# A step of plain f's put ahead of the operand building, the building cut in two, and two weight sums given to POOL

## The chip, the cores and the metric

The kernel runs on one core of one Trainium2 chip. The metric is device time of one execution in microseconds (us), lower is better. The engines are called PE (matmuls, with PEld for its weight loads), DVE (vector), ACT (activations), POOL (GpSimd) and SP (which here only issues transfers).

## The reference

Two layers of a hybrid block on one sequence of 1024 tokens, 1024 features, in float32. A layer has a mixing part with four mixers side by side and a feed-forward part with a gate:

```python
def conv_ffn(h, w_up, conv_w, conv_b, w_down):
    a, b = jnp.split(h @ w_up, 2, axis=-1)
    a = causal_dwconv(a, conv_w) + conv_b.astype(a.dtype)
    return (jax.nn.gelu(a, approximate=True) * b) @ w_down

def hybrid_layer(x, ...):
    h = rms_norm(x, g_pre_mix)
    p = h @ w_in
    ...
    y = jnp.concatenate([y_a, y_b, y_c, y_d], axis=-1).astype(dt)
    x = x + rms_norm(y @ w_out, g_post_mix)
    h = rms_norm(x, g_pre_ffn)
    x = x + rms_norm(conv_ffn(h, w_up, conv_w, conv_b, w_down), g_post_ffn)
    return x
```

`D_FF` is 2816, which is 22 groups of 128 columns, called f's below (0 to 21).

## The kernel before, in words

**Precision.** A float32 operand x is kept as two reduced-precision tiles, hi = cast(x) (ACT) and lo = x - hi (DVE). A product is three matmuls: hi·hi, hi·lo and lo·hi.

**Tiles and halves.** The sequence is worked on in two halves of 512 tokens, each of 4 blocks of 128. Half 0 (the first) of a stage runs while half 1 is prepared, and so on. Instructions are written in a Python order, but a scheduler of the framework gives each engine its order at build time; each engine then works through its list strictly in that order and waits where a semaphore asks for it. Each DMA queue belongs to an engine and is in the engine's list: SP's holds weight loads and most stores, POOL's holds the loads `hn`, the stores to `hnD` and `gD`, and some norms' loads.

**The end of layer 1.** This is the place of the change. `out(l, 1, y, True)` is the second half's output projection (L235 to L237 are its matmuls), followed block by block by the norms (`norms`, L316 to L326). The tiles of the four blocks are called oqf, okt, org and osu. For each block: load of the residual `xb`, square and mean on ACT (`sumsq`, L309), a chain of nine small DVE operations for the inverse root (L280 to L288), L319 (scale), L320 (add to `xb`), a store of `xb` to `xs` by SP (L321), once more square and root, and L324, which gives the rows for the feed-forward part; POOL stores them to `hnD` (L326).

**The feed-forward part of the last layer** has two forms. Half 0 of f's 0 to 9 is done the plain way, by `plain_part`, a generator: each step does two f's (four weight units through `a_unit`, 24 matmuls each, L214 to L216, then gate and split), and the down products of the step before (`down`, 48 matmuls, L1054 to L1056, with the additions L1061); a sixth step does the last down products. One step is taken in the last mixing stage, `NMIX = 2` more before `out`, and the other three after the operands of half 1 are built.

The rest is done by products in Strassen's manner (Winograd's form, 7 products in place of 8): `build` makes the operands of one half from the stored rows. It works in two portions (`pairs` 0 and 1), each of two blocks: two loads `hn` (L1128), four sums on POOL (`sums`, L1103 to L1106, into `sa` and `sb`), 28 transposes on PE (L1112, four for each of the seven operands A11, S1, S2, A12, S3, Q4, A22), and for each operand a cast on ACT (L1118) and a subtraction on DVE (L1119). The tiles `hn`, `sa`, `sb` and the passes' `a` and `c` share one tag `c` with four buffers. `up_f(l, f, halves)` is a pass of one f over one half (84 matmuls, L1139, called a half-pass here) or over both (168, a full pass). It loads two weight tiles (`wraw`, three buffers), makes seven casts with their subtractions (L1154, L1155) and four sums of weights (L1159), all marked as urgent (`ahead=2000`), multiplies, gates (L1207 to L1212), and stores the gated row to `gD` by POOL (L1213). The f's 10 to 21 take full passes; f's 0 to 9 need half-passes for half 1 only. Before, f's 0 and 1 run, then both portions of half 0 are built, and the other eight half-passes stand between full ones.

Of the kernel before, what the change touches and what calls it, by code (L numbers as in the profile page):

```python
# [14 lines left out]
ALU = mybir.AluOpType  # L15
# [11 lines left out]
NF = 22  # L27
# [27 lines left out]
NA = 14  # L55
WS = 1056
FULL = (1,)
NPRE, NMIX = 10, 2

PM_DCW, PM_PSC, PM_SLG, PM_DNG, PM_ALOG, PM_DT, PM_PBD = 0, 24, 26, 28, 29, 33, 37  # L60
PM_N = 37 + 256
# [57 lines left out]
class Net:  # L119
# [1023 lines left out]
    def up_f(self, l, f, halves, ahead=2000):  # L1143
        nc, pf = self.nc, self.pf[l]
        V, cf = nc.vector, self.state[l]["cf"]
        n = len(halves)
        N = 256 * n
        rb, ra = (self.pu.tile([P, 2, 512], F32, tag="raw", name="wraw", bufs=3) for _ in range(2))
        for e, r in ((1, rb), (0, ra)):
            nc.sync.dma_start(r.rearrange("p q c -> p (q c)"), self.t["wU"][l, 2 * f + e])  # L1150

        def cast(x):
            w = self.pv.tile([P, 2, 512], F32R, tag="w", name="w", bufs=9)
            nc.scalar.copy(w[:, 0], x)  # L1154
            V.tensor_tensor(w[:, 1], x, w[:, 0].bitcast(F32), ALU.subtract)  # L1155
            return w

        def add(o, a):
            V.tensor_tensor(o, o, a, ALU.add)  # L1159

        with self.tc.high_priority(offset=ahead):
            b11, b21, b12, b22 = rb[:, 0], rb[:, 1], ra[:, 0], ra[:, 1]
            w11 = cast(b11)
            add(b11, b12)
            wt1 = cast(b11)
            w22 = cast(b22)
            add(b12, b22)
            add(b22, b11)
            wt2 = cast(b22)
            w21 = cast(b21)  # L1170
            wt3 = cast(b12)
            add(b21, b22)
            wt4 = cast(b21)
        X = self.ps()[:, :N]
        Z = self.pq()[:, :N]
        W = self.pq("h")[:, :N]
        p1, p5, u2 = (self.pbuf(x)[:, :N] for x in ("p1", "p5", "u2"))
        ab = self.cbuf("a")
        a = ab[:, 0:2 + 2 * N]
        c = self.cbuf("c")[:, :2 * N]  # L1180
        at = a[:, 2:].rearrange("p (b e t) -> p b e t", b=2 * n, e=2)
        ct = c.rearrange("p (b e t) -> p b e t", b=2 * n, e=2)
        v = lambda x: x.rearrange("p (b t) -> p b t", b=2 * n)
        w = lambda j: pf[:, PF_CW + 3 * f + j:PF_CW + 3 * f + j + 1]
        cb = pf[:, PF_CB + f:PF_CB + f + 1]
        if halves[0] == 0:
            nc.gpsimd.memset(a[:, 0:2], 0.0)
        else:
            nc.gpsimd.tensor_copy(a[:, 0:2], cf[:, f, :])
        self.product(X, "A11", w11, halves, True, False)  # L1190
        self.product(Z, "S1", wt1, halves, True, False)
        with self.tc.high_priority(offset=1500):
            nc.scalar.copy(p1, X)
            nc.scalar.copy(p5, Z)
        self.product(X, "S2", wt2, halves, False, False)
        self.product(W, "A12", w21, halves, True, True)
        with self.tc.high_priority(offset=1500):
            nc.scalar.copy(u2, X)
            V.tensor_tensor(p1, p1, W, ALU.add)
        self.product(X, "S3", wt3, halves, False, False)  # L1200
        self.product(Z, "Q4", w22, halves, False, True)
        with self.tc.high_priority(offset=1500):
            V.tensor_tensor(at[:, :, 1], v(p5), v(X), ALU.subtract)
            V.tensor_tensor(at[:, :, 0], v(Z), v(u2), ALU.subtract)
        self.product(X, "A22", wt4, halves, False, True)
        with self.tc.high_priority(offset=1500):
            nc.scalar.activation(c, a[:, 2:], AF.Identity, bias=cb, scale=w(2))  # L1207
            V.scalar_tensor_tensor(c, a[:, 1:1 + 2 * N], w(1), c, ALU.mult, ALU.add)
            V.scalar_tensor_tensor(c, a[:, 0:2 * N], w(0), c, ALU.mult, ALU.add)
            nc.scalar.activation(c, c, AF.Gelu_apprx_tanh)  # L1210
            V.tensor_tensor(ct[:, :, 0], ct[:, :, 0], v(p1), ALU.mult)
            V.tensor_tensor(ct[:, :, 1], ct[:, :, 1], v(X), ALU.mult)  # L1212
        nc.gpsimd.dma_start(self.gD[l][f, :, halves[0] * HALF:halves[0] * HALF + 2 * N], c)  # L1213

    def down_full(self, l):
        nc, t = self.nc, self.t
# [140 lines left out]
    def run(self):  # L1357
        hT = self.first_norm(0)
        y = self.win(0, 0, hT)
        hT = self.hT1  # L1360
        pre = self.early(0, 1, hT)
        acc = self.out(0, 0, y, halves=True)
        y = self.win(0, 1, hT, pre)
        for l in range(DEPTH - 1):
            acc = self.ffn_norm(l, 0, self.ffn(l, 0, self.to_hT(acc, True)))
            self.load_params(l + 1)
            hT = self.to_hT(acc)
            acc = self.out(l, 1, y)
            y = self.win(l + 1, 0, hT)
            acc = self.ffn_norm(l, 1, self.ffn(l, 1, self.to_hT(acc, True)))  # L1370
            hT = self.to_hT(acc)
            acc = self.out(l + 1, 0, y)
            keep = {}

            def fill(a=acc):
                keep["g"] = self.plain_part(l + 1, self.to_hT(a, True))
                next(keep["g"])

            y = self.win(l + 1, 1, hT, mid=fill)
        l = DEPTH - 1  # L1380
        part = keep["g"]
        for _ in range(NMIX):
            next(part)
        self.out(l, 1, y, True)
        self.A = {}
        self.layout("left", ("pu", 1), ("pA1", 1))
        self.rows(self.pA1, 1)
        self.build(l, 1)
        for _ in part:
            pass  # L1390
        self.layout("right", ("pA0", 1), ("pv", 9))
        self.rows(self.pA0, 0)
        for f in range(2):
            self.up_f(l, f, (1,))
        self.build(l, 0)
        half = list(range(2, NPRE))
        for f in range(NPRE, NF):
            if half:
                self.up_f(l, half.pop(0), (1,))
            self.up_f(l, f, (0, 1))  # L1400
        self.down_phase()
        self.down_full(l)
        for st in self.stacks.values():
            st.close()
# [77 lines left out]
```

## Time and profile before

| | us |
|---|---|
| median of 3 runs (lowest, highest) | 2557.81 (2556.66, 2564.56) |
| the profiled execution | 2557.59 |
| its span, first to last instruction | 2555.8 |
| PE busy | 2435.4 (95%) |
| DVE busy | 1809.1 (71%) |
| ACT busy | 983.0 (38%) |
| POOL busy | 272.0 (11%) |

The profile cuts the span in 40 slices of 63.9 us; each digit is the busy share of a slice in tenths. Mean granted TensorE clock over the span is 0.978. In the timeline a row has start, duration, engine, line, operation, output and input, shape, and in brackets how long the engine was idle before it and what ended that. A line number with L is a line of the kernel.

### The profile page before, as it was taken

What the parts mean: (1) busy time and instruction counts of PE and PEld (TensorE: products, weight loads), DVE (VectorE), ACT (ScalarE), POOL (GpSimd) and SP (SyncE); (2) the same over time, 40 slices, a digit from 0 to 9 for tenths busy, and PEclk for the clock granted to TensorE, in tenths of its full rate; (3) what the DMA queues carried; (4) which work ended last, traced back from release to release, by engine and by line L of the source; (5) the groups of instructions that cost most, each with busy time, mean ns of one, the idle gap of its engine ahead of it and who ended that gap; (6) DMA issues with size and microseconds to landing.
All of it is one profiled execution on the core that took longest, in us unless ns stands there. A gap on an engine that the chain in (4) does not pass through costs nothing.

```text
span 2555.8 us, 38925 instructions
## 1 busy us (share of the span) xinstructions
PE 2435.4 (95%) x15220; PEld 2093.1 (82%) x15220; DVE 1809.1 (71%) x3719; ACT 983.0 (38%) x1538; POOL 272.0 (11%) x389
## 2 busy tenths in 40 slices
PE   8989998999999999999999999999949799999998
PEld 7968987877788987787788898777838699999887
DVE  7895799765655898955665689976655777774747
ACT  5333452423332553332332355234432444443412
POOL 2321113000000013100000002211020200000000
PEclk9999998999999999999999999999969899999999
DMA  5233442322223552322222354222442332222723
GB/s 182 71 89 109 131 142 82 98 76 83 79 91 124 165 163 71 91 82 76 83 91 91 128 186 149 85 84 64 165 155 78 114 101 98 96 88 80 257 67 132
DMA packets 100221, 281.00 MB, mean 110 GB/s; under 512 B 30834, under 2 KB 31154, under 8 KB 99524
## 3 DMA queue, kind: packets, MB, share of 16 engines
q1 hardware_dynamic: 91428, 248.54, 30.7%
q0 software_dynamic: 8608, 29.96, 3.4%
q8 instruction: 120, 1.97, 0.3%
q14 instruction: 65, 0.53, 0.1%
HBM read 241.20 MB, written 37.26 MB: 109 GB/s over the span
## 4 chain that ended last, share of the span: by engine, by line
PE 75%; DVE 14%; DMA 4%; issue 4%; ACT 2%; POOL 1%; SPq 0%; DVEq 0%; ACTq 0%; POOLq 0%
PE psg L215 9%; PE psg L216 9%; PE psg L214 9%; PE psg L1139 7%; PE psm L1139 4%; PE psg L1297 3%; PE psg L1298 3%; PE psg L1299 3%; DVE pr L841 3%; PE psg L235 3%; PE psg L236 3%; PE psg L237 3%; DVE wlo L205 2%; PE psh L1139 2%; DVE A L843 1%
## 5 line engine op out<-in xcount | busy, mean ns | idle before, releaser
L216 PE MATMUL psg<-hT,wlo 128*128 128x512 f32 x1312 | 524.1, 401 | 0.0
L215 PE MATMUL psg<-hT,whi 128*128 128x512 f32 x1312 | 523.4, 399 | 0.2 <-DVE hT L373 0.2
L204 ACT CAST whi<-raw 128x1024 fp32r<-128x1024 f32 (+1 forms) x290 | 301.9, 1048 | 570.6 <-PE psg L215 229.0
L214 PE MATMUL psg<-hT,whi 128*128 128x512 f32 x1312 | 518.9, 396 | 0.1
L205 DVE TENSOR_TENSOR wlo<-raw,whi 128x1024 fp32r<-128x1024 f32 (+1 forms) x267 | 329.2, 1239 | 171.5 <-ACT whi L204 166.7
L214 PEld LDWEIGHTS psg<-hT,whi 128*128 128x128 f32 x1312 | 250.4, 191 | 56.5 <-ACT tmp L436 0.5
L215 PEld LDWEIGHTS psg<-hT,whi 128*128 128x128 f32 x1312 | 247.8, 189 | 57.9 <-DVE hT L373 0.8
L216 PEld LDWEIGHTS psg<-hT,wlo 128*128 128x128 f32 x1312 | 247.5, 189 | 53.7 <-issue 0.4
L1304 DVE TENSOR_TENSOR acc<-acc,psg 128x512 f32<-128x512 f32 x160 | 109.1, 686 | 72.7 <-PE psg L1299 72.1
L236 PE MATMUL psg<-wlo,hT 128*128 128x256 f32 (+1 forms) x512 | 149.9, 294 | 7.2 <-DVE wlo L205 5.7
L235 PE MATMUL psg<-whi,hT 128*128 128x256 f32 (+1 forms) x512 | 147.1, 291 | 3.2 <-ACT tmp L436 1.9
L237 PE MATMUL psg<-whi,hT 128*128 128x256 f32 (+1 forms) x512 | 149.2, 292 | 0.0
L235 PE MATMUL psg<-whi,y 128*128 128x256 f32 x512 | 142.8, 285 | 5.8 <-ACT whi L204 3.1
L1154 ACT CAST w<-wraw 128x512 fp32r<-128x512 f32 x154 | 91.4, 620 | 143.5 <-PE psg L1139 74.9
L236 PE MATMUL psg<-wlo,y 128*128 128x256 f32 x512 | 143.6, 283 | 0.8 <-DVE rv L297 0.8
L237 PE MATMUL psg<-whi,y 128*128 128x256 f32 x512 | 143.7, 284 | 0.0
L1297 PE MATMUL psg<-whi,g 128*128 128x512 f32 x352 | 140.2, 400 | 0.0
L1298 PE MATMUL psg<-wlo,g 128*128 128x512 f32 x352 | 138.8, 394 | 0.0
L1299 PE MATMUL psg<-whi,g 128*128 128x512 f32 x352 | 138.0, 392 | 0.0
L1155 DVE TENSOR_TENSOR w<-wraw,w 128x512 fp32r<-128x512 f32 x154 | 103.2, 695 | 37.4 <-ACT w L1154 37.1
L841 DVE SCALAR_TENSOR_TENSOR pr<-A 64x1 f32<-64x1 f32 (+30 forms) x124 | 110.2, 889 | 9.8 <-POOL A L837 7.5
L236 PEld LDWEIGHTS psg<-wlo,hT 128*128 128x128 f32 x512 | 99.5, 194 | 11.3 <-DVE wlo L205 6.4
(472 smaller groups left out, 5158.9 us busy)
## 6 DMA issues: line engine op xcount, KB each, us to landing
raw<-in_wU SPq DMA_DIRECT2D x108, 512.0 KB, 3.4
raw<-in_wA SPq DMA_DIRECT2D x56, 512.0 KB, 3.8
raw<-in_wD SPq DMA_DIRECT2D x54, 512.0 KB, 3.5
wraw<-in_wU SPq DMA_DIRECT2D x44, 512.0 KB, 3.4
raw<-in_wO SPq DMA_DIRECT2D x40, 512.0 KB, 3.7
raw<-in_wB SPq DMA_DIRECT2D x24, 512.0 KB, 3.7
xs<-xb SPq DMA_DIRECT2D x24, 512.0 KB, 3.3
wraw<-in_wD SPq DMA_DIRECT2D x22, 512.0 KB, 4.6
```

The lines of the kernel that those rows point to most:

```text
L204: nc.scalar.copy(hi[:, :n], raw[:, :n])
L205: eng.tensor_tensor(lo[:, :n], raw[:, :n], hi[:, :n].bitcast(F32), ALU.subtract)
L214: nc.tensor.matmul(ps, a[0], b[0], start=first, stop=False)
L215: nc.tensor.matmul(ps, a[0], b[1], start=False, stop=False)
L216: nc.tensor.matmul(ps, a[1], b[0], start=False, stop=last)
L235: self.nc.tensor.matmul(ps[:, :width], h0, hi[:, s], start=k == 0, stop=False)
L236: self.nc.tensor.matmul(ps[:, :width], h0, lo[:, s], start=False, stop=False)
L237: self.nc.tensor.matmul(ps[:, :width], h1, hi[:, s], start=False, stop=k == len(hT) - 1)
L1139: self.nc.tensor.matmul(ps[:, 256 * j:256 * j + 256], b[:, x, s], self.A[h][n][y][:, k, :], start=first and k == i == j == 0, stop=k == 3 ...
L1297: nc.tensor.matmul(ps, hi[:, tb], us[i][0][:, s], start=i == 0, stop=False)
L1298: nc.tensor.matmul(ps, hi[:, tb], us[i][1][:, s], start=False, stop=False)
L1299: nc.tensor.matmul(ps, lo[:, tb], us[i][0][:, s], start=False, stop=i == len(g0) - 1)
```

## The change

There are three parts. One step of `plain_part` is taken between `out` and the build of half 1 (`NCOVER = 1`), so two instead of three are left for after the build. The build of half 0 comes one half-pass later and is written in two calls, a portion after three half-passes and the other after a fourth; six half-passes instead of eight are then left to stand between full passes. And in every half-pass (n == 1) the second and the fourth sum of weights go to POOL; the full passes keep all four on DVE. The code of `run` from this place on moves to a method `up_all`.

```diff
-NPRE, NMIX = 10, 2
+NPRE, NMIX, NCOVER = 10, 2, 1
...
-        def add(o, a):
-            V.tensor_tensor(o, o, a, ALU.add)
+        def add(o, a, eng=V):
+            eng.tensor_tensor(o, o, a, ALU.add)
+
+        G = nc.gpsimd if n == 1 else V
...
-            add(b12, b22)
+            add(b12, b22, G)
             add(b22, b11)
...
-            add(b21, b22)
+            add(b21, b22, G)
...
+    def up_all(self, l, y, part):
+        for _ in range(NMIX):
+            next(part)
+        self.out(l, 1, y, True)
+        for _ in range(NCOVER):
+            next(part)
+        self.A = {}
+        self.layout("left", ("pu", 1), ("pA1", 1))
+        self.rows(self.pA1, 1)
+        self.build(l, 1)
+        for _ in part:
+            pass
+        self.layout("right", ("pA0", 1), ("pv", 9))
+        self.rows(self.pA0, 0)
+        for f in range(3):
+            self.up_f(l, f, (1,))
+        self.build(l, 0, (0,))
+        self.up_f(l, 3, (1,))
+        self.build(l, 0, (1,))
+        half = list(range(4, NPRE))
+        for f in range(NPRE, NF):
+            if half:
+                self.up_f(l, half.pop(0), (1,))
+            self.up_f(l, f, (0, 1))
```

Below is what stands on the engines at three places, before and then after. In brackets are the engines or DMA queues whose semaphores an instruction waits for.

First ACT, from the last weight cast after the output projection. `xb_17432` belongs to block 3, `xb_17471` and `osu` to block 4. Before:

```order
L204 CAST whi_17724<-raw_17723 128x1024 [waits DMAHW1_49,DVE_49]
L309 ACTIVATE sq_17453,ss_17454<-xb_17432 128x1024 [waits DVE_49,Activation_49]
L309 ACTIVATE sq_17473,ss_17474<-osu_16837 128x1024 [waits Activation_49]
L309 ACTIVATE sq_17492,ss_17493<-xb_17471 128x1024 [waits DVE_49,Activation_49]
L1118 CAST A11h1_17519<-psg_17543 128x4x128 [waits PE_49]
```

After, from the second square of that list; L1029 and L1037 are the gate of the step put ahead, `whi` its weight casts and those of the step behind it:

```order
L309 ACTIVATE sq_17473,ss_17474<-osu_16837 128x1024 [waits Activation_49]
L204 CAST whi_17654<-raw_17653 128x1024 [waits DMAHW4_49,PE_49]
L209 CAST g_17579<-c_17510 128x512 [waits DVE_49]
L204 CAST whi_17660<-raw_17659 128x1024 [waits DMAHW6_49,PE_49]
L1029 ACTIVATE c_17510<-psg_17588,pf1_7912 128x512 [waits PE_49]
L1031 COPY cf1_7937<-psg_17588 128x2
L204 CAST whi_17872<-raw_17871 128x1024 [waits DMAHW7_49,PE_49]
L309 ACTIVATE sq_17492,ss_17493<-xb_17471 128x1024 [waits DVE_49,Activation_49]
```

Three casts that wait for PE now stand between block 4's two squares.

Next DVE at the end of block 4's norm (`rt`, `rs` are the small operations, L324 the rows to be stored). Before:

```order
L285 SCALAR_TENSOR_TENSOR rt_17496<-rs_17495 128x1 [waits DVE_49]
L286 TENSOR_TENSOR rt_17496<-rt_17496,rv_17497 128x1 [waits DVE_49]
L287 SCALAR_TENSOR_TENSOR rt_17496<-rt_17496 128x1 [waits DVE_49]
L288 SCALAR_TENSOR_TENSOR rs_17495<-rt_17496,rs_17495 128x1 [waits DVE_49]
L324 SCALAR_TENSOR_TENSOR osu_16837<-xb_17471,rs_17495,oap_16840 128x1024 [waits DVE_49]
```

After:

```order
L1061 TENSOR_TENSOR acc1_15768<-acc1_15768,psg_17689 128x512 [waits PE_49]
L284 SCALAR_TENSOR_TENSOR rs_17495<-rt_17496,rs_17495 128x1 [waits DVE_49]
L285 SCALAR_TENSOR_TENSOR rt_17496<-rs_17495 128x1 [waits DVE_49]
L286 TENSOR_TENSOR rt_17496<-rt_17496,rv_17497 128x1 [waits DVE_49]
L1061 TENSOR_TENSOR acc2_15769<-acc2_15769,psg_17697 128x512 [waits PE_49]
L287 SCALAR_TENSOR_TENSOR rt_17496<-rt_17496 128x1 [waits DVE_49]
L288 SCALAR_TENSOR_TENSOR rs_17495<-rt_17496,rs_17495 128x1 [waits DVE_49]
L324 SCALAR_TENSOR_TENSOR osu_16837<-xb_17471,rs_17495,oap_16840 128x1024 [waits DVE_49]
```

Five of the step's eight additions of down products (L1061) now stand ahead of L324, two of them seen here, each with a wait for PE.

Last POOL, around the first portion of half 0's build. Before:

```order
L1189 COPY a_18363<-cf1_7937 128x2 [waits PE_49]
L1213 DMA gD1_109<-c_18229 128x512 [waits DVE_49,Activation_49]
L1128 DMA hn_18463<-hnD1_107 128x1024 [waits Pool_49]
L1128 DMA hn_18465<-hnD1_107 128x1024 [waits DMASW5_49]
L1103 TENSOR_TENSOR sa_18467<-hn_18465 128x512 [waits DVE_49,DMASW7_49,Activation_49,Pool_49]
```

After (L1159 on POOL are the sums of weights; L1215 is L1213 of before):

```order
L1159 TENSOR_TENSOR wraw_18464<-wraw_18464 128x512 [waits DVE_49,DMAHW1_49,Activation_49,Pool_49]
L1215 DMA gD1_109<-c_18364 128x512 [waits DVE_49,Activation_49]
L1159 TENSOR_TENSOR wraw_18463<-wraw_18463,wraw_18464 128x512 [waits DMAHW0_49,DVE_49]
L1128 DMA hn_18598<-hnD1_107 128x1024
L1128 DMA hn_18600<-hnD1_107 128x1024 [waits DMASW6_49,PE_49]
L1159 TENSOR_TENSOR wraw_18658<-wraw_18658 128x512 [waits DVE_49,DMAHW3_49,Activation_49,Pool_49]
L1103 TENSOR_TENSOR sa_18602<-hn_18600 128x512 [waits DMASW0_49,DVE_49,Activation_49]
L1215 DMA gD1_109<-c_18499 128x512 [waits DVE_49,Activation_49]
```

The two loads stand behind both sums of the third half-pass and the store of the second one's gated row; the fourth half-pass's first sum is ahead of the portion's first sum.

More of the change, by code (lines that the diff above doesn't have):

```diff
@@ L1380, in run @@
         l = DEPTH - 1
[L1381 to L1400, printed above, removed]
+        self.up_all(l, y, keep["g"])
         self.down_phase()
```

## The prediction

> **What bounds the kernel now.** I read the forty slices first, then busy times in stretches cut at the seams of the end of the mixing layer, then the timelines of the engines in the two stretches where PE is not full.
>
> ```profile
> PE   8989998999999999999999999999949799999998
> PEclk9999998999999999999999999999969899999999
> ```
>
> PE is full nearly everywhere; two slices stand out, the 30th and the 32nd, and both lie where this change works. The next view cuts them. Columns: stretch, length, busy us of PE, PEld, DVE, ACT, POOL with counts, granted clock, DMA share, GB/s.
>
> ```profile
> 1857.62:1887.13 29.51, 0.00 (x0) 0.00 (x1) 16.49 (x50) 6.10 (x11) 2.66 (x5) 0.58 0.72 247
> 1887.13:1906.64 19.51, 13.03 (x57) 11.22 (x58) 8.49 (x13) 7.62 (x13) 11.46 (x12) 0.59 0.17 57
> 1906.64:1951.30 44.66, 44.66 (x195) 36.38 (x194) 21.71 (x27) 13.11 (x19) 0.00 (x0) 1.00 0.26 83
> 1951.30:1984.30 33.00, 33.00 (x144) 26.65 (x143) 18.76 (x25) 7.27 (x10) 0.00 (x0) 1.00 0.21 77
> 1984.30:2010.40 26.10, 21.87 (x169) 20.22 (x167) 21.69 (x38) 12.52 (x25) 1.49 (x3) 1.00 0.38 127
> 2010.40:2037.09 26.69, 13.79 (x73) 10.90 (x72) 20.57 (x29) 11.57 (x22) 13.31 (x14) 0.74 0.36 117
> 2140.00:2250.00 110.00, 110.00 (x932) 110.00 (x931) 84.99 (x133) 50.90 (x87) 6.81 (x14) 1.00 0.28 92
> ```
>
> Row 1: the second output projection has ended, PE does nothing for 29.51 us while the last norms run. Row 2: the second half's operands are built (56 transposes), PE idle for 6.5 us. Rows 3 and 4: the last three steps of plain f's, PE full. Row 5: two half-passes, 4.2 us idle. Row 6: the first half's operands, 12.9 us idle. Row 7: half- and full passes in turn, PE full and DVE at 85 of 110 us. So there are three holes of 29.5 + 6.5, 4.2 and 12.9 us, and elsewhere only PE's work counts.
>
> **The first hole.** What PE waits for:
>
> ```profile
> 1861.15 1.04 ACT L204 CAST whi<-raw 128x1024 fp32r<-128x1024 f32 x1 [1.66 <-DMA raw<-in_wU]
> 1864.71 1.28 DVE L319 SCALAR_TENSOR_TENSOR org<-org,rs,ozf 128x1024 f32<-128x1024 f32 x1
> 1872.72 1.28 DVE L319 SCALAR_TENSOR_TENSOR osu<-osu,rs,ozf 128x1024 f32<-128x1024 f32 x1
> 1875.36 1.06 ACT L309 ACTIVATE sq<-xb 128x1024 bf16<-128x1024 f32 x1 [5.68 <-DVE xb L320]
> 1878.46 1.29 DVE L324 SCALAR_TENSOR_TENSOR osu<-xb,rs,oap 128x1024 f32<-128x1024 f32 x1
> 1880.27 0.53 POOL L326 DMA_DIRECT2D hnD<-osu  x1 [7.18 <-issue]
> 1880.88 1.05 POOL L1128 DMA_DIRECT2D hn<-hnD  x2
> 1887.13 1.12 PE L1112 MATMUL psg<-ident,hn 128*128 128x128 f32 x4 [29.51 <-DMA hn<-hnD]
> ```
>
> The norms of blocks 3 and 4 (org, osu) end at 1879.75. POOL stores block 4's rows, and behind that store in its queue stand the loads of blocks 1 and 2 for the build. From the end of L324 to the first transpose: 1887.13 - 1879.75 = 7.4 us.
>
> What the change puts there, one step of plain f's, is counted from these rows (64 x 3 + 48 x 3 matmuls in 1906.64 to 1984.30):
>
> ```profile
> L214 PE MATMUL psg<-hT,whi 128*128 128x512 f32 x64 | 25.2, 394 | 0.0
> L1054 PE MATMUL psg<-whi,g 128*128 128x512 f32 x48 | 18.6, 394 | 0.0
> ```
>
> 336 matmuls in 77.66 us are 0.231 us each. The step moved ahead has 96 of the one kind and 48 of the other: 144 x 0.231 = 33.3 us. Its first three weight units are already cast at 1862.2 (first row of the fence before), so PE can start at 1857.62 with hardly a wait. If nothing else moved, the whole 33.3 us would be gained, since the 29.51 us of waiting would be covered and 3.8 us would delay the build.
>
> But the step brings ACT and DVE work that the order puts between the pieces of the last norm. Durations:
>
> ```profile
> L1029 ACT ACTIVATE c<-psg,pf x10: 772/775/802, 1690.4 to 1957.5; 128x512 f32<-128x512 f32 x10
> L1032 DVE SCALAR_TENSOR_TENSOR c<-psg,pf,c x10: 742/744/747, 1692.0 to 1958.7; 128x511 f32<-128x511 f32 x10
> L1061 DVE TENSOR_TENSOR acc<-acc,psg x32: 677/687/689, 1797.1 to 1984.5; 128x512 f32<-128x512 f32 x32
> ```
>
> I walk it. A weight unit is 24 matmuls, 5.55 us, so PE's four units end at 1863.2, 1868.7, 1874.3 and 1879.8. On ACT the square of block 4 (1875.36 before) now stands behind the cast of a fifth unit, whose buffer comes free only when the fourth unit ends: the cast runs to about 1881.4, the square to 1882.6. On DVE the nine small operations of that block's norm stand between five additions of down products (L1061), each waiting for PE. The gelu behind that square ends at 1883.3, the gating product at about 1884.4, and until then the third down group's PSUM buffer is held (1.8 us of PE lost; the normal start would be 1882.6), the fifth group ends at 1884.4 + 3 x 1.39 = 1888.6, its addition at 1889.5, two small operations follow, and L324 ends near 1891.1 instead of 1879.75: 11.4 us later. POOL's store and loads move along, and the first transpose comes at 1898.5, after an idle of 5.8 us (the down groups end at 1892.7). The build keeps its 19.5 us, its pace being set by loads and POOL sums. So the stage after it starts 11.4 us later and has 33.3 us less to do: **-21.9 us**. Bounds: no delay of the norm, -33.3; a delay half as long again (17 us), -16. SP's queue moves too: block 4's store of xs goes behind two weight loads; it is read again only at the end, so it costs nothing. The load of the fifth unit needs a buffer free at 1873 and lands before 1878.
>
> **The second stage.** Before, two half-passes and then both portions of the build; after, three, a portion, one, a portion. The rows:
>
> ```profile
> 1996.69 0.69 DVE L1159 TENSOR_TENSOR wraw<-wraw 128x512 f32<-128x512 f32 x1 [0.80 <-DMA wraw<-in_wU]
> 2004.37 1.73 SPq L1150 DMA_DIRECT2D wraw<-in_wU  x2
> 2007.90 0.69 DVE L1159 TENSOR_TENSOR wraw<-wraw 128x512 f32<-128x512 f32 x1 [0.70 <-DMA wraw<-in_wU]
> wraw<-in_wU SPq DMA_DIRECT2D x44, 512.0 KB, 3.4
> 2021.39 1.25 POOL L1105 TENSOR_TENSOR sb<-sa,hn 128x512 f32<-128x512 f32 x1 [2.21 <-DMA gD<-c]
> 2022.69 1.12 PE L1112 MATMUL psm<-ident,sb 128*128 128x128 f32 x4 [4.53 <-POOL sb L1105]
> ```
>
> A half-pass has 84 matmuls; 932 in 110 us are 0.118 each, so PE needs 9.9 us. Yet the first sum of weights repeats every 11.2 us (1996.69 to 2007.90): the buffer for the next pass's second load is free only after the pass's last sum (the issue at 2004.37), and then 3.4 us of load follow (row 4). So a half-pass that stands alone is held by its weight chain. The build beside it is held by POOL: its third sum (row 5) first waits 2.21 us for the store of a gated row, and PE stands 4.53 us for it (last row). Now two of its four sums go to POOL. What they cost there:
>
> ```profile
> 1889.69 1.26 POOL L1106 TENSOR_TENSOR sb<-hn 128x512 f32<-128x512 f32 x1
> 2014.04 1.73 POOL L1103 TENSOR_TENSOR sa<-hn 128x512 f32<-128x512 f32 x1 [3.49 <-DVE w L1155]
> 2014.54 1.78 DVE L1159 TENSOR_TENSOR wraw<-wraw 128x512 f32<-128x512 f32 x1
> ```
>
> 1.26 us on POOL against 0.69 on DVE, and when both engines add from SBUF at once, POOL's takes 1.73 and DVE's 1.78, 1.09 us more. DVE is spared 2 x 0.69 = 1.4 us a pass and may lose up to 2 x 1.09 = 2.2. The third and fourth sum and the last cast wait for POOL, so the chain gets longer, not shorter. Bounds of the period: 11.2 (all hidden) and 13.2 (a full collision on each sum, and the chain longer by 0.6 a sum); I take the middle, 12.2.
>
> With 12.2 the third half-pass ends 38 us into the stage (252 x 0.118 = 29.8 of work, 8.2 idle against 4.2 for two). POOL issues the first portion's loads only after that pass's last sum, at 35, landing near 40; sums and stores of gated rows share its queue, and the fourth pass (96 products, 28 transposes) ends near 61.5 with 5.5 us idle. The second portion's loads wait in POOL's queue behind both sums of the fifth pass, so 2.5 us more are idle. 16.2 us of idle against 4.2 + 12.9 = 17.1: **-1 us**. Bounds: the build hidden and no collision, -13; period 13.2 and the build's idle as before, +6.
>
> The later passes: two half-passes fewer are paired with full ones. In pairs PE is full with DVE at 77%; the twelve POOL sums there add at most 12 x (1.09 - 0.69) = 5 us of DVE in 180. Nothing, as long as PE stays the slower one.
>
> **Sum.** 2557.6 (the profiled execution, 0.2 below the median) - 21.9 - 1.0 = 2534.7 us.
>
> **Rivals.** (a) The last norm slips in between early and the first stage gains all 33.3: 2557.6 - 33.3 - 1 = 2523. For it: DVE is busy only 16.5 of 29.5 us in the hole. Against it: the order, in which ACT meets the square only after a cast that waits for PE. (b) The second portion of the change works as the words say and hides the build: 12 us more, 2523 as well. Against it: POOL issues the loads late. (c) Slower: POOL's queue becomes the brake in the pairs. There, the second sum of each of six half-passes stands behind the store of the half-pass before it, which waits for that pass's gating. If each made PE wait 5 us or more (6 x 5 = 30), 22.9 would be lost and more: 2565. It decides once PE idles 3.8 us a pair. Against it: a full pass of 19.9 us lies between that gating and the need. (d) Each POOL sum blocks DVE in full, as in the one collision above: the period is 13.2, three passes are 1 us longer each and the fourth as well, 2534.7 + 4 = 2539. For it: most DVE work of a half-pass adds or subtracts two SBUF tiles. Against it: DVE idles in part of each period. By a rule of the Trainium skill (SBUF — State Buffer, section SBUF: two separate sides) this is how it must go, since a DVE operation with two SBUF inputs and a GpSimd operation that reads SBUF lock each other out of one port for the whole instruction; the collision agrees with it, 1.09 us for the loser. (e) The step put ahead does not cover: its weights come late and PE idles between units, so that half the gain goes: 2546. Against it: loads land in 3.5 us and a unit lasts 5.55.
>
> **Chances.** The forecast 0.38; (a) 0.10, (b) 0.12, both together 0.02 (2511); (d) 0.20; (e) 0.12; (c) 0.03; no change for a cause I don't see 0.03. The range 2521 to 2547 holds the forecast, (a), (b), (d) and most of (e); it leaves out both together, (c), no change and the ends of the bounds. A change under 0.3% (7.7 us) can't be told from none here: faster 0.92, same 0.05, slower 0.03.
>
> **What would show it.** Right: in the profile after, the slice with PE at 4 is gone; PE runs plain f's straight from the projection's end; an idle of about 6 us before the first transpose, released by the load of hn; L324 of osu ending some 11 us later than now; the plain f's ending near 1962; three half-passes at about 12 us apiece; POOL sums of 1.3 to 1.7 us on wraw; the last transpose near 2034. Wrong: if the square of block 4 starts before 1878, the first term is too small; if PE idles in the stretch of pairs, the second is wrong in sign.

## The result, and the profile after

The changed kernel takes 2538.34 us, median of 4 runs (2536.66 to 2539.80), against 2557.23 of the kernel before, median of 4 (2551.70 to 2564.56). The ratio is 0.9924, 95% interval 0.9898 to 0.9950: 19 us faster, where 2534.7 was forecast. The profiled execution took 2536.66 us (span 2534.9), 20.9 less than the one of before.

The slices of PE and of its granted clock after the change:

```profile
PE   8989998999999999999999999989988799999998
PEclk9999999999999999999999999999999999999999
```

The 4 of before and the two low clocks beside it (slices 30 and 32) are gone. What is left are an 8 in slices 30 and 31, in which the first of the two stages lies, and a 7 in slice 32, which is in the second. The stretches after the change (length, busy us of PE, PEld, DVE, ACT, POOL with counts, granted clock, DMA share, GB/s):

```profile
1855.85:1889.60 33.75, 33.74 (x146) 26.85 (x144) 29.64 (x70) 14.43 (x24) 2.28 (x5) 1.00 0.58 206
1889.60:1895.21 5.61, 0.01 (x1) 0.03 (x1) 2.96 (x3) 1.35 (x2) 0.37 (x1) 0.96 0.96 294
1895.21:1914.70 19.49, 12.44 (x57) 10.64 (x58) 8.28 (x13) 7.45 (x14) 11.27 (x11) 0.59 0.41 154
1914.70:1959.30 44.60, 44.60 (x193) 36.06 (x193) 22.52 (x30) 10.25 (x15) 0.00 (x0) 0.99 0.20 69
1959.30:1998.20 38.90, 32.71 (x242) 30.50 (x240) 28.74 (x47) 17.61 (x35) 11.82 (x12) 0.96 0.33 112
1998.20:2036.50 38.30, 24.66 (x166) 22.71 (x167) 31.84 (x46) 19.23 (x37) 19.67 (x18) 0.82 0.34 123
2036.50:2332.70 296.20, 296.20 (x2506) 296.20 (x2505) 200.47 (x297) 126.67 (x206) 24.67 (x44) 1.00 0.26 86
```

Row 1 is the moved step: PE, which stood still here for 29.51 us, is full from the projection's end. Row 2 is what the step doesn't cover. Row 3, the second half's build, is as before. Rows 5 and 6 are the half-passes that stand alone and the first half's build: 38.90 - 32.71 = 6.2 us idle until the third half-pass ends, and 38.30 - 24.66 = 13.6 us in the fourth and the two portions. Row 7: PE is full from the last transpose to the last product.

Totals of single executions differ by several us for reasons that have nothing to do with the change (the end of the output projection alone lies between 1852.8 and 1860.5 us in the profiles below). So all kernels are compared by stage: A, from the output projection's end to the first product of a half-pass; B, from there to the last product of the passes of `up_f` (L1139; in brackets the time to the last transpose of the first half's build, which lies in it); C, from there to the end of the span. They are read from each profile's timeline, so each is of one execution. Us; the names of the experiments are explained where each is told.

| kernel | median | ratio to before, 95% interval | A | B (to last transpose) | C |
|---|---|---|---|---|---|
| before | 2557.23 | | 126.8 | 368.9 (52.8) | 202.6 |
| after | 2538.34 | 0.9924, 0.9898 to 0.9950 | 103.5 | 373.5 (77.1) | 202.2 |
| 1 cover only | 2534.07 | 0.9916, 0.9899 to 0.9932 | 101.6 | 367.6 (51.5) | 202.8 |
| 2 sums on DVE | 2538.20 | 0.9930, 0.9917 to 0.9943 | 103.0 | 374.1 (80.2) | 202.3 |
| 3 POOL sums only | 2556.69 | 1.0006, 0.9993 to 1.0018 | 125.0 | 368.6 (52.5) | 202.3 |
| 4 split only | 2562.46 | 1.0016, 1.0006 to 1.0026 | 126.5 | 372.0 (78.1) | 204.5 |
| 5 split, own buffers | 2524.94 | 0.9876, 0.9855 to 0.9897 | 102.5 | 357.0 (50.5) | 206.1 |
| 6 cover only, own buffers | 2520.49 | 0.9857, 0.9835 to 0.9878 | 103.1 | 354.4 (36.8) | 202.8 |
| 7 two steps | 2521.51 | 0.9861, 0.9841 to 0.9880 | 93.0 | 370.2 (54.1) | 202.2 |
| 8 after, own buffers | 2525.73 | 0.9888, 0.9862 to 0.9913 | 101.7 | 360.4 (54.1) | 204.2 |
| 9 two steps, own buffers | 2512.89 | 0.9818, 0.9792 to 0.9843 | 93.9 | 355.2 (37.3) | 205.9 |
| 10 before, own buffers | 2540.62 | 0.9940, 0.9919 to 0.9961 | 126.4 | 356.0 (38.5) | 204.0 |
| 11 three steps, own buffers | 2518.55 | 0.9852, 0.9820 to 0.9884 | 96.6 | 358.6 (42.8) | 206.4 |

Of the 20.9 us between the two profiles, 1.6 lie ahead of the change, A gives 23.4, B takes 4.5 back, C gives 0.4. A went as forecast, B did not: there a gain of 1.0 was forecast.

The end of the last norm after the change (timeline rows of ACT, DVE, POOL and PE):

```profile
1878.09 1.05 ACT L204 CAST whi<-raw 128x1024 fp32r<-128x1024 f32 x1 [3.77 <-PE psg L215]
1879.05 1.05 ACT L309 ACTIVATE sq<-xb 128x1024 bf16<-128x1024 f32 x1
1880.98 0.68 DVE L1038 TENSOR_TENSOR c<-c,psg 128x512 f32<-128x512 f32 x1
1886.49 1.28 DVE L324 SCALAR_TENSOR_TENSOR osu<-xb,rs,oap 128x1024 f32<-128x1024 f32 x1
1888.30 0.53 POOL L326 DMA_DIRECT2D hnD<-osu  x1 [13.38 <-issue]
1888.91 1.05 POOL L1128 DMA_DIRECT2D hn<-hnD  x2
1895.21 1.09 PE L1112 MATMUL psg<-ident,hn 128*128 128x128 f32 x4 [5.60 <-DMA hn<-hnD]
```

The square of block 4 (second row) stands behind a weight cast that waits for PE (first row). Block 4's rows are ready 8.0 us later than before, counted from the start of the execution, and 9.6 later counted from the projection's end (1886.49 - 1855.85 = 30.6 against 1878.46 - 1857.46 = 21.0). PE waits 5.60 us for the loads, which stand behind the store of block 4's rows in POOL's queue.

The second stage after the change: the first sum of weights of each of four half-passes, one collision of POOL and DVE, and what PE waits for in the build:

```profile
1960.82 0.69 DVE L1159 TENSOR_TENSOR wraw<-wraw 128x512 f32<-128x512 f32 x1
1972.43 0.69 DVE L1159 TENSOR_TENSOR wraw<-wraw 128x512 f32<-128x512 f32 x1 [0.67 <-DMA wraw<-in_wU]
1985.02 0.69 DVE L1159 TENSOR_TENSOR wraw<-wraw 128x512 f32<-128x512 f32 x1 [1.05 <-DMA wraw<-in_wU]
1998.01 0.69 DVE L1159 TENSOR_TENSOR wraw<-wraw 128x512 f32<-128x512 f32 x1
...
1973.36 1.57 POOL L1159 TENSOR_TENSOR wraw<-wraw 128x512 f32<-128x512 f32 x1 [4.29 <-DVE wraw L1159]
1973.81 1.67 DVE L1155 TENSOR_TENSOR w<-wraw,w 128x512 fp32r<-128x512 f32 x1
...
2005.59 0.58 PE L1139 MATMUL psh<-A12h,w 128*128 128x256 f32 x1 [5.31 <-ACT w L1154]
2027.00 0.63 PE L1112 MATMUL psg<-ident,hn 128*128 128x128 f32 x4 [2.52 <-DMA hn<-hnD]
2031.96 1.11 PE L1112 MATMUL psm<-ident,sa 128*128 128x128 f32 x4 [4.33 <-POOL sa L1103]
```

The half-passes are 11.6, 12.6 and 13.0 us apart, and POOL and DVE do collide. The largest of PE's waits, 5.31 us, is the fourth half-pass's, for a weight cast, in a stretch in which DVE is full (13.30 of the 13.62 us from 1996.08 to 2009.70). The other two are the second portion's, for its loads and its first sum. It looks as if the sums on POOL cost what B lost. The experiments show that B is as long without them.

### The profile page after: what moved, and what is told of

Read it like the earlier page. It is cut to its first block, busy times and chain, and to the rows that moved or that the text cites. A ratio compares the mean times of both kernels' runs of the same rounds, so it can differ in the third digit from the quotient of the medians.

```text
span 2534.9 us, 38970 instructions
## 1 busy us (share of the span) xinstructions
PE 2430.8 (96%) x15220; PEld 2088.1 (82%) x15220; DVE 1802.9 (71%) x3699; ACT 981.7 (39%) x1538; POOL 298.8 (12%) x409
## 4 chain that ended last, share of the span: by engine, by line
PE 73%; DVE 15%; DMA 4%; issue 4%; ACT 3%; POOL 1%; SPq 0%; DVEq 0%; ACTq 0%; POOLq 0%
PE psg L215 9%; PE psg L216 9%; PE psg L214 9%; PE psg L1139 7%; PE psm L1139 4%; PE psg L1324 3%; PE psg L1325 3%; PE psg L1326 3%; DVE pr L841 3%; PE psg L236 3%; PE psg L235 3%; PE psg L237 3%; DVE wlo L205 2%; PE psh L1139 2%; DVE A L843 2%
## 5 line engine op out<-in xcount | busy, mean ns | idle before, releaser
L1155 DVE TENSOR_TENSOR w<-wraw,w 128x512 fp32r<-128x512 f32 x154 | 108.5, 728 | 38.8 <-ACT w L1154 37.7
L236 PEld LDWEIGHTS psg<-wlo,hT 128*128 128x128 f32 x512 | 98.2, 192 | 11.4 <-DVE wlo L205 6.8
```

The source lines that it names most:

```text
L236: self.nc.tensor.matmul(ps[:, :width], h0, lo[:, s], start=False, stop=False)
```

## The experiments

### First series: which of the three parts costs what

Theory: the whole gain is that of the moved step, and POOL's sums take something back in the half-passes, by collisions. Rival: the cut of the build in two costs it, whoever makes the sums.

**1, cover only.** The kernel after with the other two parts undone:

```diff
-        G = nc.gpsimd if n == 1 else V
+        G = V
...
-        for f in range(3):
+        for f in range(2):
             self.up_f(l, f, (1,))
-        self.build(l, 0, (0,))
-        self.up_f(l, 3, (1,))
-        self.build(l, 0, (1,))
-        half = list(range(4, NPRE))
+        self.build(l, 0)
+        half = list(range(2, NPRE))
```

> The step of plain f's put ahead of the build, and nothing else: half 0 is built whole after two half-passes and all sums stay on DVE, as before. Theory: the first stage gives all of the gain (in the profile after, PRODUCTS of the second stage start 23.2 us earlier counted from the end of the output projection), and the second stage takes 52.8 us as before; 2557.2 - 23.2 = 2534 us, so about 4 us faster than the changed kernel. Rival: the split and the POOL sums carry part of the gain; then this kernel is slower than the changed one, 2541 us or more.

Measured: 2534.07 us; A 101.6, B 367.6. The moved step alone gives the whole gain of A, and B is as before. The other two parts together cost 5.9 us of B and bring nothing in A.

**2, sums on DVE.** The kernel after with only the sums put back:

```diff
-        G = nc.gpsimd if n == 1 else V
+        G = V
```

> The changed kernel with all four sums of weights back on DVE: the step ahead and the split building stay. Theory: POOL's sums are what lengthens the half-passes (first weight sums 11.6, 12.6 and 13.0 us apart after, 11.2 before); here they are 11.2 apart again, and the second stage, 77.1 us after, takes 77.1 - 4.5 = 72.6 or less; 2534 us. Rival: the sums on POOL are harmless and the split itself costs the 4.5 us, because a third and fourth half-pass run at the pace of their weight chain; then the second stage stays at 76 to 78 us and the time at 2538.

Measured: 2538.20 us, and the ratio is that of the kernel after (0.9930 against 0.9924). B is 374.1: the loss stays with no sum on POOL. The half-passes do get shorter, 11.0 us apart on average where they were 12.4 (the first sums of the first and the fourth start at 1959.69 and 1992.79), but PE idles 21.1 us to the last transpose in place of 19.8.

**3, POOL sums only.** The kernel before with two sums of each half-pass on POOL, so without the first two parts (`NCOVER = 0`, the build unsplit after two half-passes).

> The kernel before with only the two sums of each half-pass moved to POOL. Theory: two lone half-passes get 1.4 us longer each and the build meets POOL's sums in its queue, so the second stage takes 56 to 60 us in place of 52.8, 2560 to 2564 us; the passes in turn with full ones cost nothing (PE stays full from the last transpose on). Rival: DVE, relieved by 1.4 us a pass, gets faster and the stage shrinks to 50 us or less, 2554 us.

Measured: 2556.69 us, ratio 1.0006 (0.9993 to 1.0018); B 368.6 against 368.9. The sums on POOL cost nothing that can be measured. The theory that they take the time back fell, and so did the rival that a relieved DVE shortens the stage (to 50 us or less, measured 52.5).

**4, split only.** The kernel before with only the build cut in two (`NCOVER = 0`, `G = V`).

> The kernel before with only half 0's building split, a portion after three half-passes and one after a fourth; all sums on DVE, no step ahead. Theory: the split hides part of the build's 12.9 us idle but runs one or two more half-passes at 11.2 us in place of 9.9; the second stage takes 68 to 73 us for its 168 products more, where 72.6 would be no gain; 2553 to 2558 us. Rival: the split is what costs the second stage; 76 to 78 us, 2561 us.

Measured: ratio 1.0016 (1.0006 to 1.0026), B 372.0: 3.1 us more than before. The cut is a small loss by itself. The rival holds.

### What holds the build: the ring of four buffers

In the kernel with all sums on DVE POOL has only the build's own work and the stores of gated rows, and its timeline shows what each step waits for:

```profile
1990.30 0.55 POOL L1215 DMA_DIRECT2D gD<-c  x1 [10.36 <-ACT w L1154]
1990.84 0.54 POOL L1128 DMA_DIRECT2D hn<-hnD  x1
1996.77 0.55 POOL L1128 DMA_DIRECT2D hn<-hnD  x1 [5.39 <-DMA gD<-c]
2000.82 1.27 POOL L1103 TENSOR_TENSOR sa<-hn 128x512 f32<-128x512 f32 x1 [3.50 <-DVE c L1214]
2002.17 1.60 POOL L1104 TENSOR_TENSOR sa<-sa,hn 128x512 f32<-128x512 f32 x1
2003.71 0.57 POOL L1215 DMA_DIRECT2D gD<-c  x1
2007.58 1.58 POOL L1105 TENSOR_TENSOR sb<-sa,hn 128x512 f32<-128x512 f32 x1 [3.30 <-issue]
...
2026.21 1.49 POOL L1103 TENSOR_TENSOR sa<-hn 128x512 f32<-128x512 f32 x1 [10.96 <-DVE c L1211]
```

A load of rows waits 5.39 us for a store of gated results. The first sum's 3.50 us end with that load: it takes 3.9 us to land, by the view of the tile `hn`, which is at 2000.7, and the gating that the row names (L1214) ends in the same moment. The third sum waits 3.30 us right behind the store of the third half-pass's gated row, with no releaser named. The last row is the second portion's first sum: POOL stands idle for 10.96 us before it, until the fourth half-pass is gated (L1211), though its two loads (issued at 2014.14 and half a us later, at most 4.8 us to land) are there by 2019.5. What the first portion waits for stands in POOL's list of that kernel, the semaphores in brackets:

```
L1128 DMA hn_18598<-hnD1_107 128x1024 [waits Pool_49]
L1128 DMA hn_18600<-hnD1_107 128x1024 [waits DMASW6_49,PE_49]
L1103 TENSOR_TENSOR sa_18602<-hn_18600 128x512 [waits DVE_49,DMASW0_49,Activation_49,Pool_49]
L1104 TENSOR_TENSOR sa_18602<-sa_18602,hn_18598 128x512 [waits DMASW7_49,Pool_49]
L1215 DMA gD1_109<-c_18499 128x512 [waits DVE_49,Activation_49]
L1105 TENSOR_TENSOR sb_18603<-sa_18602,hn_18598 128x512 [waits DMASW5_49,DMASW1_49,Pool_49]
```

POOL's transfers take the queues in turn: the two loads have 7 and 0, the store behind them 1. So the last row, a sum of loaded rows, waits for that store. Neither this sum, nor the load that waits for a store, nor the second portion's sum that waits for the gating reads what it waits for. What they share with it is the tag `c`: `a` and `c` of a half-pass and `hn`, `hn`, `sa`, `sb` of a portion take turns in four buffers. Counted from pass 0: `a` and `c` of pass 2 are in buffers 0 and 1, the portion's loads in 2 and 3 (3 held `c` of pass 1, whose store must have landed), `sa` in 0 and `sb` in 1. So a portion can't make its sums before the half-pass ahead of it is gated, and its third sum not before that pass's store. The second portion meets the same of the fourth half-pass. PE's waits in the same kernel:

```profile
2009.21 1.11 PE L1112 MATMUL psm<-ident,sb 128*128 128x128 f32 x4 [4.74 <-POOL sb L1105]
2027.75 0.66 PE L1112 MATMUL psm<-ident,sa 128*128 128x128 f32 x4 [3.46 <-POOL sa L1103]
2031.38 1.12 PE L1112 MATMUL psg<-ident,sa 128*128 128x128 f32 x4 [2.54 <-POOL sa L1104]
```

Theory R: this ring is the cause. Rival L: half-passes that stand alone and POOL's late loads are. They are told apart by giving the first half's build four buffers of its own; nothing that is computed changes:

```diff
     def build(self, l, h, pairs=(0, 1)):
+        cbuf = (lambda n: self.pv.tile([P, 1028], F32, tag="b", name=n, bufs=4)) if h == 0 else self.cbuf
...
-                x = self.cbuf("hn")
+                x = cbuf("hn")
...
-            sa, sb = self.cbuf("sa"), self.cbuf("sb")
+            sa, sb = cbuf("sa"), cbuf("sb")
```

**5, split, own buffers** (experiment 2 with this edit).

> The kernel after with all weight sums on DVE, as in the run with sums on DVE, and with four buffers of its own for the first half's build (its loads and sums no longer take buffers from the ring of four that the half-passes use for their gated rows). Theory R, the shared ring is what makes the split cost: a portion's sums need not wait for the pass ahead of it to be gated and stored; PE's idle beside the two portions falls from 15 us to 4 to 8, and the stage from first to last product of the first projection falls from 374.0 us to 364 to 369. Theory L, the split costs because half-passes that stand alone are held by their weights and POOL's queue puts the loads late anyway: within 1.5 us of 374.

Measured: 2524.94 us, 13 less than experiment 2; B 357.0 against 374.1. The sums of these stretches (total, then busy us by engine), experiment 2 and experiment 5, from first to last product:

```profile
sum 374.10, PE 352.96 PEld 348.65 DVE 264.67 ACT 163.38 POOL 30.03; mean PE 176.48 PEld 174.32 DVE 132.33 ACT 81.69 POOL 15.01
```

```profile
sum 357.10, PE 348.19 PEld 344.60 DVE 265.03 ACT 163.26 POOL 31.37; mean PE 174.09 PEld 172.30 DVE 132.52 ACT 81.63 POOL 15.68
```

PE's idle falls from 374.1 - 353.0 = 21.1 us to 357.1 - 348.2 = 8.9, and its busy time for the same matmuls from 353.0 to 348.2. The second goes with the clock; the stretch from the first product to the last transpose in both, in the same order:

```profile
1958.20:2038.30 80.10, 58.96 (x427) 54.69 (x426) 63.80 (x103) 37.08 (x71) 16.33 (x20) 0.91 0.34 113
```

```profile
1958.90:2009.40 50.50, 43.70 (x347) 40.87 (x346) 47.35 (x74) 28.09 (x55) 17.30 (x19) 1.00 0.40 131
```

Granted clock 0.91 against 1.00. A wait of PE is paid twice here: once as idle time, and once as slower transposes behind it (four of them take 1.12 us instead of 0.66 in the rows above). Theory R holds, and by more than it foretold (364 to 369): it had left out the clock, 4.8 us, and the idle time fell by 12.2 us where 7 to 11 were foretold.

**6, cover only, own buffers** (experiment 1 with the same edit).

> The kernel with only the moved step of plain f's (build unsplit after two half-passes, sums on DVE), and four buffers of its own for the first half's build. Theory R: the build's 13 us of idle PE fall to 6 or less, first to last product 367.6 us becomes 359 to 363, and the time about 2527. Theory L: within 1.5 us of 367.6, time about 2534.

Measured: 2520.49 us; B 354.4 against 367.6. Again R, and again more than foretold. POOL's timeline shows the first portion of this kernel:

```profile
1970.61 1.30 POOL L1103 TENSOR_TENSOR sa<-hn 128x512 f32<-128x512 f32 x1 [7.29 <-DMA hn<-hnD]
1971.87 1.75 POOL L1106 TENSOR_TENSOR sb<-hn 128x512 f32<-128x512 f32 x1
1973.57 1.75 POOL L1104 TENSOR_TENSOR sa<-sa,hn 128x512 f32<-128x512 f32 x1
1975.40 1.60 POOL L1105 TENSOR_TENSOR sb<-sa,hn 128x512 f32<-128x512 f32 x1
```

The sums run one after the other behind the load, 9 us after the first product (1961.8), and the transposes then fill the gaps that the half-passes leave. This edit does two things at once: the waits go, and the scheduler, for which the buffers are free, lists the loads earlier (the first is issued at 1962.22, 0.5 us after the first product, and at 1983.88, 21.8 us after it, in experiment 1). They weren't taken apart; both hang on the ring. So the half of Rival L that blames POOL's late loads is not refuted: the loads were late because of the ring. Beside experiment 5 this also prices the cut with the ring out of the way: B 357.0 against 354.4, 2.6 us for two more half-passes that stand alone. With the ring the cut costs 6.5 us behind the moved step (374.1 against 367.6; 3.1 without that step, experiment 4), so 3.9 of the 6.5 are the ring's.

**8, after, own buffers** (the whole change with the edit).

> The kernel after, whole (one step moved, two portions, two sums of a half-pass on POOL), and four buffers of its own for the first half's build. Theory R: first to last product 373.4 us falls to 365 to 369, time about 2530. Theory L: within 1.5 us of 373.4, time about 2538. Were POOL's sums what holds the build in this kernel, the run with sums on DVE and own buffers would fall and this one would not.

Measured: 2525.73 us, B 360.4. R holds with the sums on POOL too. Against experiment 5, B is 3.4 us longer with them, while the times (2525.73 and 2524.94) do not differ beyond their scatter (2521.17 to 2532.08 and 2521.37 to 2528.17); whether the collisions begin to count once the build no longer waits stays open.

**10, before, own buffers** (the kernel before with the edit alone).

> The kernel before with nothing changed but four buffers of its own for the first half's build. Theory R: the ring held that build in the kernel before too, so the products go from 369 us to 353 to 358 and the time from 2557 to 2542 to 2546, with none of the three parts of the change. Theory L, or own buffers that help only behind the moved step: 2553 to 2557.

Measured: 2540.62 us, ratio 0.9940 (0.9919 to 0.9961), B 356.0 against 368.9. Four buffers give the kernel before almost what the whole change gave (the profiled execution took 2547.52; by its stages 12.9 us are the buffers'). The ring held its build too: the POOL row quoted in the prediction, `sb L1105` waiting 2.21 us for `gD<-c`, was its trace. But a brake that both kernels have does not tell why one is longer than the other: from before to after B grows by some 4.5 us with the ring (368.9 to 373.5), and by 4.4 with own buffers in both (356.0 to 360.4).

### The first stage: what the late norm leaves

**7, two steps.** Experiment 1 with `NCOVER = 2`.

> Two steps of plain f's between the second output projection and the second half's build, build of the first half unsplit, sums on DVE. If the norm of block 4, made late by the moved step, is what leaves PE idle 5.6 us before the first transpose with one step, a second step covers it: from the projection's end to the first product 101.6 us becomes 95 to 97, time 2527 to 2529. If the second step's own work delays the loads and the norm again by as much, or the build's transposes just come later with the same idle, it stays within 1.5 us of 101.6 and the time near 2534.

Measured: 2521.51 us; A 93.0 against 101.6, more than the 5 to 6 us of that idle. The stretches up to the first transpose, and from there to the first product:

```profile
1855.15:1911.95 56.80, 56.79 (x246) 45.85 (x245) 42.26 (x83) 23.21 (x36) 8.74 (x9) 1.00 0.62 214
1911.95:1948.20 36.25, 30.72 (x150) 25.34 (x149) 22.29 (x33) 10.30 (x18) 6.46 (x8) 0.91 0.19 71
```

PE runs without a gap to the first transpose. The first transposes stand between the second step's last matmuls, at the full clock:

```profile
1911.95:1926.00 14.05, 13.06 (x69) 10.61 (x67) 10.78 (x17) 5.09 (x9) 1.10 (x2) 1.00 0.01 2
```

So the step covers the idle ahead of the build (4.8 us in experiment 1), some of the build's own 7.0 (19.49 - 12.44 in the kernel after; 36.25 - 30.72 = 5.5 are left) and the slow clock of its first portion. By PE's busy time over A, 90.1 us in experiment 1 and 87.5 here, 2.6 of the 8.6 us go with the clock (0.92 and 0.96 in the mean) and the other 6.0 are idle time.

**9, two steps, own buffers.** Experiment 7 with the edit of the buffers.

> Two steps of plain f's moved ahead, first half's build unsplit after two half-passes, sums on DVE, four buffers of its own for that build. If the two cures are of different stages they add: 2557 - 36 (two steps alone) - 14 (own buffers, 2520.5 against 2534.1) = 2507, with about 93 us from the projection's end to the first product and 354 us of products. If they draw on the same idle of PE, the time stays near 2520.

Measured: 2512.89 us, ratio 0.9818 (0.9792 to 0.9843), the fastest of all: 25 us under the kernel after. A 93.9 and B 355.2: the cures add, to within a microsecond in each stage. The total is 6 above the sum. The kernel before was 2.9 us slower beside this run than beside experiment 7 (2560.16 and 2557.25), and C is 3.7 longer than in experiment 7 (205.9 against 202.2). C varies from 202.2 to 206.4 over the profiles with no edit in it. Of the 3.7 us, 3.3 are one wait of PE for a tile of ACT (`acc`, 4.5 us against 1.2); why that wait varies stays open.

**11, three steps, own buffers.**

> As the run with two steps and own buffers, but three steps moved ahead. If the second step has already covered what the late norm left, the third one has nothing to cover and only puts the build's own idle (5 us of 11) after all of plain f's: 93 us from the projection's end to the first product as with two steps, within 2 us, or longer by up to 6. If each step covers more, below 91.

Measured: 2518.55 us; A 96.6 against 93.9. The third step has nothing left to cover, and the last portion of the build has lost the plain f's that stood behind and between it. PE's rows there:

```profile
1942.76 1.09 PE L1112 MATMUL psg<-ident,hn 128*128 128x128 f32 x4 [6.26 <-DMA hn<-hnD]
1948.16 1.12 PE L1112 MATMUL psm<-ident,sa 128*128 128x128 f32 x4 [4.31 <-POOL sa L1103]
```

10.6 us of waiting in two rows, for the second portion's loads and its first sum. The first product comes at 1950.80 here, and 16 of the build's 56 transposes behind it, so a part of this build's price lies in B (358.6 against 355.2).

## Why the prediction was right, and where it was not

**The moved step (33.3 us of work, 144 x 0.231).** Right. PE is full for 33.75 us from the projection's end, and experiment 1 shows that this part alone makes the gain. Rival (e), that it wouldn't cover, fell.

**The late norm (+11.4 us).** The mechanism was right, the size a little high: L324 came 9.6 us later, counted from the projection's end. The square did stand behind the cast of a fifth unit, which waited for the fourth, as foretold. The projection ended 1.6 us earlier in the profile after; with that added to its times, the cast ended at 1880.8 for a forecast of 1881.4, the gating product (L1038) at 1883.3 for 1884.4, and L324 at 1889.4 for 1891.1. The stall of 1.8 us that the working put on the third down group did not come: PE was busy for 33.74 of the 33.75 us. So A gained 23.4 us for a forecast 21.9. The idle ahead of the first transpose was forecast at 5.8 us, was 5.60, and its releaser was the load of `hn`, as foretold. Plain f's ended at 1959.3 for a forecast of about 1962, 1.6 of it ahead of the change. Rival (a), a norm that slips in early, fell.

**The build of the second half (19.5 us, unchanged).** Right: 19.49, clock 0.59. Experiment 7, where the build begins at a granted clock of 1.00 between products, shows that neither number is the build's own.

**The second stage (-1.0 us).** This is the step that failed: B lost 4.5. Its first half was right: the period of a half-pass was forecast at 12.2 and averaged 12.4, and the third half-pass ended 38.9 us into the stage for a forecast of 38. POOL's sums on `wraw` took 1.28 to 1.67 us, as foretold. The term that was mis-sized is the idle of the build behind it: 5.5 + 2.5 = 8.0 us forecast, 13.6 measured. The last transpose was to come 71.6 us into the stage (near 2034, the stage beginning near 1962.4) and came 77.1 us into it. These 5.5 us are the distance between the gain that was forecast and the loss that was measured. (The working gives the fourth pass 96 products, where a pass has 84; as its sum goes by idle time alone, that does not reach the result.)

In the kernel after, the fourth pass and the first portion idle 6.7 us (5.31 for a weight cast, 1.40 for a copy on ACT) for a forecast of 5.5. The second portion's loads cost 2.52, as foretold. What the forecast did not have are the 4.33 us that PE then waits for this portion's first sum, which POOL makes right behind the store of the fourth half-pass's gated row (2030.07 and 2030.63). Some 1.6 us of them are that store and the gating before it; the others are the second load, which lands near 2029.0, and the sum itself. The forecast had no price for the clock either: of the 4.5 us that B lost, 1.8 are busy time of PE for the same products (353.6 us against 351.8).

The working took the place of the loads in POOL's queue for the brake, and let sums and stores of gated rows merely share that queue. It had in hand a sum of loaded rows that waits 2.21 us for a store, and did not ask why it should; the answer, one ring of four buffers, was in the code that it described. Experiments 5, 6, 8 and 10 show what the ring costs: with it taken away B falls by 13 to 17 us. They do not show that it is the whole of the loss. Of the cut's price of 6.5 us, with the sums on DVE, 3.9 are the ring's, and 2.6 stay as the price of half-passes that stand alone. With the sums on POOL the change costs B 4.4 us without the ring too, of which 3.4 lie between experiments 5 and 8, which differ by the sums alone; what makes these is not shown.

**Rival (d), 2539.** It hit the time within 1 us, and that is luck: experiments 2 and 3 show that the time is the same with and without sums on POOL. Its collisions are real: 1.57 us for 1.28 on POOL, 1.67 for 0.7 on DVE. The rule of the Trainium skill behind it (SBUF — State Buffer, section SBUF: two separate sides), an exclusive port for DVE operations with two SBUF inputs and GpSimd operations that read SBUF, agrees with those rows. It says how long an operation takes, and not whether anyone waits for it. The half-passes are 1.4 us longer with the sums on POOL (12.4 against 11.0), but in experiment 2 the time that they save is lost again in the build, where the second portion's first sum waits for the gating.

**Rival (b), the build hidden.** The idle that it hoped to hide could be hidden, but not by cutting the build: that was done by the buffers, in the kernel before and in the one after.

**The pairs (nothing).** Right: PE is full in 296.20 of 296.20 us, and rival (c) fell with it.

## What to carry to other kernels

Before a stage is reordered, follow every wait in it to its reason. Where an operation waits for something that it doesn't read, it waits for a buffer, and the move will meet the same wait again; list the tiles that share a ring in the order in which they are taken, and see whose end each one needs. In this kernel four buffers were worth 13 us of the stage, in the kernel before as in the one after; the Trainium skill (Perfetto Trace Analysis, section Optimization Strategy) says that a gap which repeats on the engine that should be full can mean too few buffers, and here the trace agrees, with PE's waits of 2.54 to 4.74 us. When a rival lands on the measured time, undo its mechanism alone before it is believed. And when a brake has been found, take it out of both kernels: only what then becomes of their difference tells how much of it the brake explains.

## What the hardware showed that had not been expected

A PE that waits in short pieces had less clock here as well. Behind an idle of 5.6 us the build of the second half ran at a granted clock of 0.59 over 19.49 us with PE busy for 64% of them, and four transposes took 1.12 us instead of 0.66. With another step up to the transposes (experiment 7) the same work began at 1.00. In the products, going from clock 0.91 to 1.00 in the build's stretch went with 4.8 us less of busy PE for the same matmuls, on top of 12.2 us less of idle.
